# A hybrid block on one core: the front of its mixer is put in another order

## The chip, the cores and the metric

The kernel runs on one core of a Trainium2 chip. The metric is the time of one execution on the device in microseconds (us), the median of several runs. Engines: TensorE (PE; PEld is its weight load), VectorE (DVE), ScalarE (ACT), GpSimd (POOL), and SyncE (SP), which here only issues DMAs. ScalarE issues DMAs too (ACTq).

## The reference

One layer over 1024 latent and 256 context tokens, width 1024, in float32: a gated feed-forward half-step, a mixer, a second half-step, a final norm. Each is modulated by nine vectors of 1024 made from the conditioning vector. The mixer, cut to what matters:

```python
p = h @ w_in                                  # latent and context tokens
# delta-net group: 4 heads of 128
qkv = silu(centred_dwconv(p[q, k, v], conv))  # 5 taps, along the tokens
q, k = l2norm(q), l2norm(k)
beta = sigmoid(p[b]); g = -exp(a_log) * softplus(p[a] + dt_bias)
o = gated_delta(q, k, v, g, beta)             # chunked, both directions
dn = rmsnorm(o) * silu(p[z])
# attention group: 4 query heads, 2 key/value heads of 128
aq, ak = rope(rmsnorm(p[q])), rope(rmsnorm(p[k]))   # latent tokens: 2-D rotation
at = softmax(aq @ ak.T / sqrt(128)) @ av
x = x + gate * (concat(dn, at) @ w_out)
```

## The kernel before

All products are float32 built from three products of rounded parts: a weight or activation is split into a high half (`whi`, `hh..`, a ScalarE copy) and a low half (`wlo`, `hl..`, a subtraction); `load_cols(..., spare=True)` does the subtraction on GpSimd. There are two buffers for raw weights and four each for halves of 128x1024, so two weight blocks of 256 columns at a time.

The program is written in one order; the framework then orders each engine's instructions by that order and its own estimate of when operands are ready. It may issue an instruction ahead of others written earlier on the same engine. Engines and SyncE's queue then work strictly in the issued order.

The front of the mixer, in program order:

1. z rows and value rows of tokens 4 to 7 (in blocks of 128; `tok_mm`, 24 matmuls into one of two `psB` buffers; `z_out` a Silu and a store, `v_out` a copy and a store).
2. `conv_pair("k", ..)`: two heads of the convolution. A head (`conv_head`) is 24 matmuls for each of two 512-token blocks and one 256-token block into `psA` (two buffers), copied to `pp`; then five taps per segment, the first on ScalarE, four on VectorE (`ac`), Silu, and for q and k a square. Later (`pump`) a matmul with ones sums the squares, and k and v are transposed (`tk`) and stored.
3. Ten rows of 272 columns: 16 columns for beta and decay (copied by VectorE to `ba`), 256 for query heads 0 and 1 (copied to `xr` by ScalarE).
4. The second k pair; small vectors.
5. Ten turns of `stage1` (the chunks' triangular matrices `s1N`, stored to `nb_d`, `nt_d`), each with key rows for attention; the four v heads of the convolution stand before the loop and after turns 2, 4 and 7.
6. Both q pairs of the convolution, with `invert` (31 steps of two VectorE instructions, then three transposing ScalarE copies `Lb` and the stores `xx_d`) beside them.
7. Eight query rows (heads 2 and 3), `invert` going on; then eight z rows, the attention keys `k_head(0)` after the fourth.
8. Four tiles (`slot`, 128x4096) are set to zero, and `stage2_load` fills their blocks from `nt_d` and `xx_d`.
9. A new PSUM pool; `attend` and the chunk recurrence `chain` take turns.

`Rope` normalizes and rotates rows: ScalarE squares each row with a scrap tile that shares its two buffers (`t2`) with the rotation, VectorE makes the reciprocal roots and scales, GpSimd rotates with a table piece `cc` loaded for each row. It works once for four rows. `leave` issues the stores.

All through the front `ml`, the modulation run, takes 64 pieces of 256 KB (`wv`, three buffers), each multiplied and summed by VectorE into `macc`; `adv(ml, n)` writes n of them.

```python
conv_pair("k", 512, 0, lambda: adv(ml, 5))
...
rope_q = Rope(gq, aq_d, 0, FOURS)
for c in (8, 9, 0, 1, 2, 3, 4, 5, 6, 7):
...
    nc.vector.tensor_copy(ba[:, c, :], pa[:, 0:16])
...
    adv(ml, 2)
...
for pr in range(2):
    conv_pair("q", 0, pr, lambda: (adv(inv, 3), leave(2)))
```

## Time and profile before

| | us |
|---|---|
| median of 3 runs (lowest, highest) | 2449.36 (2445.76, 2452.54) |
| the profiled execution's own time | 2441.68 |
| its span, first to last instruction | 2439.9 |
| TensorE busy in the span | 2340.8 |
| VectorE, ScalarE, GpSimd busy | 1747.9, 1142.8, 865.2 |
| mean granted clock of TensorE, share of full | 0.983 |

The span is what the trace covers; the profiled execution's time has 1.8 us around it. Busy times of the engines overlap. Idle time of an engine is given with what ended it.

### The profile page before, as it was taken

To read this page: it belongs to the slowest core of one execution; us is meant where nothing else is said; L and a number is where in the kernel's file an instruction comes from. 1 tells how busy PE (TensorE), PEld (TensorE's weight loads), DVE (VectorE), ACT (ScalarE), POOL (GpSimd) and SP (SyncE) were. 2 spreads that over 40 slices of the span, in tenths; PEclk is the share of its full clock that TensorE was granted. 3 is DMA by queue.
4 is the path that set the end of the run, shared out by engine and by line. 5 is a ranking of instruction groups with operands and counts; after the bars stand their busy time and mean duration, and the time that the engine had idled before them with its cause. 6 is when DMAs were issued, how large, how long until landed. Compare 5 with 4: busy or idle time off the path is not lost. (4 is left out here: it accounts for less than half of the span.)

```text
span 2439.9 us, 35896 instructions
## 1 busy us (share of the span) xinstructions
PE 2340.8 (96%) x12917; PEld 1999.4 (82%) x12917; DVE 1747.9 (72%) x2741; ACT 1142.8 (47%) x2244; POOL 865.2 (35%) x715
## 2 busy tenths in 40 slices
PE   8999999999999999998998999899999999999998
PEld 5999788877788879877877798778877888878887
DVE  4689757887777875666777566886596546677786
ACT  4485633333343464366733754565573334234345
POOL 0000244446623342245524344521134444662330
PEclk9999999999999999999998999999999999999999
DMA  9966434345554446454433456621343234555332
GB/s 303 309 215 213 150 121 156 126 158 191 179 184 130 143 158 198 152 158 130 132 107 123 116 148 198 217 102 53 106 149 119 94 134 155 177 179 168 131 128 87
DMA packets 344976, 377.80 MB, mean 155 GB/s; under 512 B 73579, under 2 KB 249375, under 8 KB 344415
## 3 DMA queue, kind: packets, MB, share of 16 engines
q1 hardware_dynamic: 298576, 320.03, 40.6%
q10 hardware_dynamic: 46223, 55.49, 6.9%
q8 instruction: 102, 1.67, 0.3%
q14 instruction: 75, 0.61, 0.1%
HBM read 283.41 MB, written 92.01 MB: 154 GB/s over the span
## 5 line engine op out<-in xcount | busy, mean ns | idle before, releaser
L407 PE MATMUL psw<-xo,uhi 128*128 128x512 f32 x1536 | 487.5, 394 | 10.3 <-ACT k L46 5.4
L407 PEld LDWEIGHTS psw<-xo,uhi 128*128 128x128 f32 x1536 | 289.8, 189 | 77.9 <-ACT k L46 6.5
L407 PE MATMUL psw<-slot,uhi 128*128 128x512 f32 x1024 | 320.8, 391 | 3.7 <-DVE nk L49 3.4
L407 PE MATMUL psw<-xo,ulo 128*128 128x512 f32 x768 | 302.6, 394 | 0.0
L49 DVE TENSOR_TENSOR ulo<-wr,uhi 128x512 fp32r<-128x512 f32 (+1 forms) x272 | 212.1, 802 | 73.6 <-ACT uhi L46 72.9
L49 POOL TENSOR_TENSOR R<-wr 128x512 f32<-128x512 f32 (+1 forms) x68 | 98.3, 1456 | 379.7 <-DMA wr<-in_ffn_w 343.3
L407 PEld LDWEIGHTS psw<-slot,uhi 128*128 128x128 f32 x1024 | 193.1, 189 | 45.8 <-issue 4.2
L46 ACT ACTIVATE uhi<-wr 128x512 fp32r<-128x512 f32 (+1 forms) x272 | 150.5, 597 | 127.1 <-PE psw L407 85.3
L407 PE MATMUL psw<-slot,ulo 128*128 128x512 f32 x512 | 200.2, 391 | 0.0
L407 PEld LDWEIGHTS psw<-xo,ulo 128*128 128x128 f32 x768 | 144.9, 189 | 32.2
L52 DVE SCALAR_TENSOR_TENSOR macc<-wv,cs,macc 128x512 f32<-128x512 f32 x140 | 134.9, 982 | 39.5 <-DMA wv<-in_w_mod 38.5
L55 PE MATMUL psA<-hc,whi 128*128 128x256 f32 x832 | 154.0, 284 | 2.3 <-ACT sil L46 2.3
L49 POOL TENSOR_TENSOR ext<-wr 128x512 f32<-128x512 f32 (+1 forms) x68 | 95.7, 1417 | 154.6 <-DMA wr<-in_ffn_w 134.4
L46 ACT ACTIVATE whi<-wr 128x1024 fp32r<-128x1024 f32 x100 | 104.3, 1054 | 89.9 <-PE pd L55 28.2
L55 PEld LDWEIGHTS psA<-hc,whi 128*128 128x128 f32 x832 | 130.8, 191 | 3.5 <-ACT sil L46 2.6
L55 PE MATMUL psA<-hc,wlo 128*128 128x256 f32 x416 | 118.2, 284 | 7.6 <-POOL wlo L49 7.6
L49 DVE TENSOR_TENSOR wlo<-wr,whi 128x1024 fp32r<-128x1024 f32 x82 | 100.2, 1234 | 27.9 <-ACT whi L46 25.8
L49 DVE TENSOR_TENSOR ulo<-ext,uhi 128x512 fp32r<-128x512 f32 (+1 forms) x102 | 96.9, 978 | 28.9 <-ACT uhi L46 28.0
L407 PEld LDWEIGHTS psw<-slot,ulo 128*128 128x128 f32 x512 | 96.5, 188 | 20.1
L46 ACT ACTIVATE k<-k 128x512 f32<-128x512 f32 x57 | 36.0, 632 | 158.6 <-DVE k L49 158.6
L52 DVE SCALAR_TENSOR_TENSOR ac<-pp,cols,ac 128x1024 f32<-128x1024 f32 (+1 forms) x80 | 84.8, 1071 | 34.2 <-ACT ac L46 33.1
L49 DVE TENSOR_TENSOR k<-psw,k 128x512 f32<-128x512 f32 x114 | 76.8, 683 | 44.2 <-PE psw L407 42.7
(485 smaller groups left out, 6277.3 us busy)
## 6 DMA issues: line engine op xcount, KB each, us to landing
wr<-in_ffn_w SPq DMA_DIRECT2D x174, 512.0 KB, 5.2
wv<-in_w_mod SPq DMA_DIRECT2D x128, 256.0 KB, 3.2
R<-gda ACTq DMA_DIRECT2D x74, 256.0 KB, 4.7
wr<-in_ffn_w SPq DMA_DIRECT2D x32, 384.0 KB, 4.9
wr<-in_w_in SPq DMA_DIRECT2D x22, 512.0 KB, 4.4
gs<-gdb ACTq DMA_DIRECT2D x43, 256.0 KB, 4.6
gda<-gt SPq DMA_DIRECT2D x40, 256.0 KB, 2.1
gdb<-gt SPq DMA_DIRECT2D x40, 256.0 KB, 2.6
```

The source lines that it names most:

```text
L46: return nc.scalar.activation(out, in_, func, **kw)
L49: return (eng or nc.vector).tensor_tensor(out=out, in0=a, in1=b, op=op)
L52: return nc.vector.scalar_tensor_tensor(out=out, in0=a, scalar=s, in1=b, op0=op0, op1=op1)
L55: nc.tensor.matmul(out, l, r, start=start, stop=stop)
L407: nc.tensor.matmul(banks[u][key], l[:, u, k, :], r_, start=new and i == 0, stop=i == 3 * pr.kq - 1, skip_group_check=True)
```

## The change

It puts the front into another order. z rows of tokens 4 to 7 come before the value rows, and all weight loads stand earlier in the program. The second set of z rows stands between the two q pairs, the query rows of heads 2 and 3 last. Attention keys, the first query block and the zeros are written between those query rows. The rotation table stays in SBUF (half as wide, cosine and sine once per pair). `ba` is copied by ScalarE, the squares get a scrap tile of their own, two of the four zero tiles are written by ScalarE as copies with scale 0, and the value low halves of head 0 are made by VectorE. `tc.keep_in_program_order` holds each sum of `ml` behind the VectorE instruction written before it, and `beat` writes one after taps 0 and 2 of each segment.

```diff
-    aq_d = [dr.tile([P, 512], F32, name=f"aq_d{c}") for c in range(8)]
+    aq_d = [[dr.tile([P, 256], F32, name=f"aq_d{c}_{i}") for c in range(8)] for i in range(2)]
...
-                    stt(acc[b], wr, c_, acc[b], ALU.mult, ALU.add)
+                    pin(stt(acc[b], wr, c_, acc[b], ALU.mult, ALU.add))
...
+    rope = rp.tile([P, 8, 2, 64], F32, name="rope")
+    nc.sync.dma_start(rope, A["rope"])
...
-            junk = rp.tile([P, P], F32, tag="t2", name="sq", bufs=2)
+            junk = rp.tile([P, P], F32, tag="sq", name="sq")
...
-                    cc = rp.tile([P, 2, P], F32, tag="cc", name="cc", bufs=4)
-                    nc.sync.dma_start(cc, A["rope"][c].rearrange("j p e -> p j e"))
-                    t2 = rp.tile([P, 2, 64, 2], F32, tag="t2", name="t2", bufs=2)
+                    t2 = rp.tile([P, 2, 64, 2], F32, tag="t2", name="t2")
                     xv = xn.rearrange("p h (e w) -> p h e w", w=2)
-                    sv = cc[:, 1, :].rearrange("p (e w) -> p e w", w=2)
+                    co, si = (rope[:, c, i, :] for i in range(2))
                     for w in range(2):
-                        tt(t2[:, :, :, w], xv[:, :, :, 1 - w], sv[:, :, w].unsqueeze(1).to_broadcast([P, 2, 64]), ALU.mult, nc.gpsimd)
-                    tt(xn, xn, cc[:, 0:1, :].to_broadcast([P, 2, P]), ALU.mult, nc.gpsimd)
-                    tt(xn, xn, t2.rearrange("p h e w -> p h (e w)"), ALU.add, nc.gpsimd)
+                        tt(t2[:, :, :, w], xv[:, :, :, 1 - w], si.unsqueeze(1).to_broadcast([P, 2, 64]), ALU.mult, nc.gpsimd)
+                    tt(xv, xv, co.unsqueeze(1).unsqueeze(3).to_broadcast([P, 2, 64, 2]), ALU.mult, nc.gpsimd)
+                    for w, op in enumerate((ALU.subtract, ALU.add)):
+                        tt(xv[:, :, :, w], xv[:, :, :, w], t2[:, :, :, w], op, nc.gpsimd)
...
-    ml = mod_run([(q, (0,)) for q in range(10, 18)], 2, lambda: m1.tile([P, 512], F32, tag="wv", name="wv", bufs=3))
+    ml = mod_run([(q, (0,)) for q in range(10, 18)], 2, lambda: m1.tile([P, 512], F32, tag="wv", name="wv", bufs=3), tc.keep_in_program_order)
...
+                if tap in (0, 2):
+                    beat()
...
     for c in range(4, 8):
         z_out(c, tok_mm(hsel, W_z, c, 256)[:, 0:256], 0)
+    Wk0 = conv_load(512, 0)
+    for c in range(4, 8):
         v_out(c, tok_mm(hsel, W_v, c, 256)[:, 0:256])
...
-    conv_pair("k", 512, 0, lambda: adv(ml, 5))
...
+    Wk1 = conv_load(512, 1)
+    conv_pair("k", 0, Wk0, beat=lambda: adv(ml, 1))
+    W = load_cols(w_in, 2576, spare=True)
...
-        nc.vector.tensor_copy(ba[:, c, :], pa[:, 0:16])
+        act(ba[:, c, :], pa[:, 0:16], AF.Copy)
...
-    conv_pair("k", 512, 1, lambda: adv(ml, 5))
+    conv_pair("k", 1, Wk1, beat=lambda: adv(ml, 1))
+    Wv = conv_load(1024, 0)
...
-    W = load_cols(w_in, 2576, spare=True)
-    heads = []
-    for pr in range(2):
-        heads.extend(conv_heads("v", 1024, pr))
+    heads = conv_heads("v", 0, Wv, lambda: adv(ml, 1))
     before = None
-    heads.pop(0)()
     for c in range(10):
...
-        if c in (2, 4, 7):
+        if c in (0, 3, 5, 8):
             heads.pop(0)()
+        if c == 3:
+            heads = conv_heads("v", 1, conv_load(1024, 1), lambda: adv(ml, 1))
+        if c == 8:
+            Wq0 = conv_load(0, 0)
         adv(ml, 2)
+    Wz = load_cols(w_in, 1792, spare=True)
...
-    for pr in range(2):
-        conv_pair("q", 0, pr, lambda: (adv(inv, 3), leave(2)))
+    conv_pair("q", 0, Wq0, lambda: (adv(inv, 3), leave(2)))
+    Wq1 = conv_load(0, 1)
...
+    for c in range(8):
+        z_rows(c)
+        adv(inv, 2 if c % 4 else 1)
+        if c in (2, 5):
+            pump()
+    Wq = load_cols(w_in, 2320, spare=True)
+    conv_pair("q", 1, Wq1, lambda: (adv(inv, 3), leave(2)))
...
-        eng.memset(sl, 0.0)
+        if eng is nc.scalar:
+            for i in range(4):
+                act(sl[:, i, :].rearrange("p (a b) -> p a b", b=P), ones.unsqueeze(1).to_broadcast([P, 8, P]), AF.Copy, scale=0.0)
+        else:
+            eng.memset(sl, 0.0)
...
+    q0 = const.tile([P, 4, P], F32R, tag="wm", name="q0", bufs=3)
+    for c in range(8):
         leave()
         rope_q(c, tok_mm(hsel, Wq, c, 256)[:, 0:256])
...
+        if c == 0:
+            adv(inv, 3)
+            pump()
+        if c == 1:
+            run(inv)
...
+            flush()
...
+            clear(1, nc.scalar)
+            clear(3, nc.gpsimd)
+        if c == 2:
+            stage2_load(0, 2, 0)
...
+            k0 = k_head(0, lambda n: krs.pop(0), [(c, 2) for c in range(0, 10, 2)], lambda: pst("Y"), ep_tiles())
+        if c == 3:
+            q0 = q_prep(0, 0, lambda: pst("Y"), (q0[:, 0:2, :], q0[:, 2:4, :]))
+            clear(0, nc.scalar)
+            clear(2, nc.gpsimd)
+    leave(9)
     stage2_load(0, 2, 1)
...
-            split_copy(wide(0, c0, n), wide(1, c0, n), vr, nc.gpsimd)
+            split_copy(wide(0, c0, n), wide(1, c0, n), vr, nc.gpsimd if kv else None)
```

`q_prep` now takes the PSUM buffer and the place of its result, and for the first block loads by SyncE; `conv_load(c0, pr)` is `load_cols(w_in, c0 + pr * 256, spare=True)`.

## Rows read from the trace of the kernel before

**Rows 1.** The page's first part: busy us, share, instructions.
```profile
PE 2340.8 (96%) x12917; PEld 1999.4 (82%) x12917; DVE 1747.9 (72%) x2741; ACT 1142.8 (47%) x2244; POOL 865.2 (35%) x715
```
**Rows 2.** By stretches: us, busy PE, PEld, DVE, ACT, POOL; clock; DMA.
```profile
936.00:1341.40 405.40, 370.46 (x2299) 330.54 (x2297) 273.95 (x430) 196.37 (x428) 163.82 (x185) 0.95 0.47 142
1341.40:1357.60 16.20, 12.39 (x47) 8.15 (x48) 8.96 (x21) 11.74 (x30) 8.38 (x6) 0.79 0.70 134
```
**Rows 3.** TensorE's waits, 936 to 1358: us in total, times, longest.
```profile
PE psA L55 <- POOL wlo L49: 7.6, 4, 5.5
PE psY L55 <- ACT pp L46: 5.1, 2, 3.9
PE psY L1394 <- DVE kl L49: 4.1, 1, 4.1
...
PE pS L55 <- ACT qh L46: 3.4, 1, 3.4
PE psB L55 <- ACT xr L46: 3.1, 2, 2.2
...
PE psB L55 <- ACT th L46: 2.8, 1, 2.8
PE psA L55 <- ACT pp L46: 2.3, 1, 2.3
```
**Rows 4.** ScalarE's waits, 936 to 1342.
```profile
ACT sq L46 <- POOL xr L49: 21.3, 5, 9.1
ACT xr L46 <- DVE ba L1188: 19.8, 7, 5.1
```
**Rows 5.** VectorE's waits, 936 to 1342.
```profile
DVE macc L52 <- DMA wv<-in_w_mod: 30.4, 24, 7.3
```
**Rows 6.** Waits of SyncE's queue, 936 to 1342.
```profile
SPq L1067 <- POOL xr L49: 89.3, 12, 65.0
```
**Rows 7.** GpSimd in order of time, 955 to 994: start, us, what, idle before.
```profile
955.81 10.95 POOL L49 TENSOR_TENSOR wlo<-wr,whi 128x1024 fp32r<-128x1024 f32 x4 [26.07 <-ACT whi L46]
```
**Rows 8.** ScalarE's groups, 936 to 1342: count, busy us, mean ns, idle before.
```profile
L46 ACT ACTIVATE whi<-wr 128x1024 fp32r<-128x1024 f32 x18 | 18.8, 1052 | 6.4 <-PE psA L55 4.7 <-PE psB L55 1.1 <-issue 0.6
L46 ACT ACTIVATE sq<-xr 128x128 f32<-128x128 f32 x52 | 15.9, 306 | 22.1 <-POOL xr L49 21.3
...
L46 ACT ACTIVATE xr<-psB 128x256 f32<-128x256 f32 x26 | 9.8, 378 | 39.6 <-DVE ba L1188 19.8 <-PE psB L55 19.8
...
L46 ACT ACTIVATE Lb<-Xb 128x1024 f32<-128x1024 f32 x2 | 3.9, 2009 | 0.0
```
**Rows 9.** ScalarE in order of time, 1335 to 1343: a z row's Silu.
```profile
1337.12 0.38 ACT L46 ACTIVATE th<-psB 128x256 f32<-128x256 f32 x1 [2.50 <-PE psB L55]
```
**Rows 10.** GpSimd's groups, 936 to 1345.
```profile
L49 POOL TENSOR_TENSOR t<-xr,cc 128x128 f32<-128x128 f32 x48 | 28.1, 597 | 86.8 <-issue 42.3 <-DVE xr L52 29.6 <-ACT ac L46 14.8
L49 POOL TENSOR_TENSOR xr<-xr,t 128x256 f32<-128x256 f32 x24 | 21.4, 891 | 0.5
```
**Rows 11.** VectorE's groups, 936 to 1342.
```profile
L52 DVE SCALAR_TENSOR_TENSOR ac<-pp,cols,ac 128x1024 f32<-128x1024 f32 x48 | 67.2, 1400 | 22.6 <-ACT ac L46 22.2
L52 DVE SCALAR_TENSOR_TENSOR macc<-wv,cs,macc 128x512 f32<-128x512 f32 x56 | 55.3, 988 | 31.0 <-DMA wv<-in_w_mod 30.4
L52 DVE SCALAR_TENSOR_TENSOR ac<-pp,cols,ac 128x256 f32<-128x256 f32 x32 | 18.5, 577 | 11.6 <-ACT ac L46 10.9
...
L1380 DVE MEMSET slot<- 128x4096 f32 x2 | 6.9, 3472 | 1.6 <-DMA ldq<-aq_d 0.8 <-DMA z_d<-th 0.8
```
**Rows 12.** VectorE in order of time, 1323 to 1343.
```profile
1323.66 0.17 DVE L1059 TENSOR_SCALAR ssc<-ssc 128x8 f32<-128x8 f32 x1 [7.73 <-ACT sq L46]
...
1326.92 4.01 DVE L52 SCALAR_TENSOR_TENSOR xr<-xr,rsc,gq 128x128 f32<-128x128 f32 x8
```
**Rows 13.** One v head's matmuls alone, by stretches (columns of rows 2 without GpSimd).
```profile
1111.50:1125.50 14.00, 13.92 (x72) 11.74 (x72) 0.00 (x0) 0.99 (x2) 1.00 0.50 144
```
**Rows 14.** VectorE in order of time, 954 to 985.
```profile
956.79 11.30 DVE L52 SCALAR_TENSOR_TENSOR macc<-wv,cs,macc 128x512 f32<-128x512 f32 x5 [0.71 <-DMA wv<-in_w_mod]
```

More of the change, by code (lines that the diff above doesn't have):

```diff
@@ L214, in mod_vec, with mod_run @@
             tt(mods[:, b, 4 * q : 4 * q + 4], red, cols1[:, off["b_mod"] + 4 * q : off["b_mod"] + 4 * q + 4], ALU.add)
-    def mod_run(qs, ahead=2, home=lambda: const.tile([P, 512], F32, tag="wm", name="wv", bufs=3)):
+    def mod_run(qs, ahead=2, home=lambda: const.tile([P, 512], F32, tag="wm", name="wv", bufs=3), pin=lambda i: i):
         todo_ = [(q, bs, k) for q, bs in qs for k in range(KT)]
@@ L1162, in conv_heads, with conv_pair @@
         return [lambda f=f: head(f) for f in range(2)]
-    def conv_pair(kind, c0, pr, then=lambda: None):
-        for fn in conv_heads(kind, c0, pr):
+    def conv_pair(kind, pr, W, then=lambda: None, beat=lambda: None):
+        for fn in conv_heads(kind, pr, W, beat):
             fn()
@@ L1398, in k_head, with q_load, q_prep @@
         return kh, kl
-    def q_load(kv, t):
+    def q_load(kv, t, eng=None):
         ld = ep.tile([P, 2, P], F32, tag="ldq", name="ldq", bufs=3)
-        nc.scalar.dma_start(ld.rearrange("p h e -> p (h e)"), aq_d[t][:, kv * 256 : kv * 256 + 256])
+        (eng or nc.scalar).dma_start(ld.rearrange("p h e -> p (h e)"), aq_d[kv][t])
         return ld
-    Wq = load_cols(w_in, 2320, spare=True)
-    rope_q = Rope(gq, aq_d, 256, FOURS)
-    def q_rows(c):
+    def q_prep(kv, t, new_ps, home=None):
+        qh, ql = home or (ap_.tile([P, 2, P], F32R, tag=nm, name=nm, bufs=2) for nm in ("qh", "ql"))
+        ld = q_load(kv, t, nc.sync if home else None)
+        pt = new_ps()
+        for j in range(2):
+            nc.tensor.transpose(pt[:, j * P : (j + 1) * P], ld[:, j, :], ident)
+        split_copy(qh, ql, pt[:, 0:256].rearrange("p (h e) -> p h e", h=2))
+        return qh, ql
@@ L1410, in q_rows @@
+    rope_q = Rope(gq, aq_d[1], FOURS)
+    q0 = const.tile([P, 4, P], F32R, tag="wm", name="q0", bufs=3)
+    for c in range(8):
         leave()
         rope_q(c, tok_mm(hsel, Wq, c, 256)[:, 0:256])
-    def z_rows(c):
-        z_out(c, tok_mm(hsel, Wz, c, 256)[:, 0:256], 256)
-    for c in range(4):
-        q_rows(c)
-        adv(inv, 5)
-        pump()
-    run(inv)
-    Wz = load_cols(w_in, 1792, spare=True)
-    es_m3.close()
-    es_hc.close()
-    slots, es_slots = open_pool("slots", side="right")
@@ L1425, in block_kernel @@
-    slot_pool = {1: slots, 3: slots}
-    for c in range(4, 8):
-        q_rows(c)
-    clear(1, nc.vector)
-    clear(3, nc.gpsimd)
-    stage2_load(0, 2, 0)
-    flush()
-    es_m1.close()
-    slots_b, es_slots_b = open_pool("slots_b", side="right")
-    slot_pool.update({0: slots_b, 2: slots_b})
-    clear(0, nc.vector)
-    clear(2, nc.gpsimd)
-    stage2_load(0, 2, 1)
-    ep, es_ep = open_pool("ep", side="right")
-    for c in range(8):
-        z_rows(c)
-        if c > 1:
-            leave()
-        if c == 3:
-            k0 = k_head(0, lambda n: ep.tile([P, 2, P], F32, tag="ldq", name="kr", bufs=3).rearrange("p c e -> p (c e)"), [(c, 2) for c in range(0, 10, 2)], lambda: pst("Y"), ep_tiles())
+        if c == 0:
+            adv(inv, 3)
+            pump()
@@ new lines, in block_kernel @@
+        if c == 1:
+            run(inv)
+            es_m3.close()
+            es_hc.close()
+            flush()
+            es_m1.close()
+            slots, es_slots = open_pool("slots", side="right")
+            slots_b, es_slots_b = open_pool("slots_b", side="right")
+            slot_pool = {1: slots, 3: slots, 0: slots_b, 2: slots_b}
+            ep, es_ep = open_pool("ep", side="right")
+            clear(1, nc.scalar)
+            clear(3, nc.gpsimd)
+        if c == 2:
+            stage2_load(0, 2, 0)
+            krs = [rp.tile([P, 256], F32, tag="zt", name="kr", bufs=3) if i < 3 else ep.tile([P, 2, P], F32, tag="ldq", name="kr", bufs=3).rearrange("p c e -> p (c e)") for i in range(5)]
+            k0 = k_head(0, lambda n: krs.pop(0), [(c, 2) for c in range(0, 10, 2)], lambda: pst("Y"), ep_tiles())
@@ L1625, in kv_head @@
             nc.scalar.dma_start(vr.rearrange("p (c e) -> p c e", e=P), av_d[c0 : c0 + n, :, kv * P : (kv + 1) * P].rearrange("c p e -> p c e"))
-            split_copy(wide(0, c0, n), wide(1, c0, n), vr, nc.gpsimd)
+            split_copy(wide(0, c0, n), wide(1, c0, n), vr, nc.gpsimd if kv else None)
         return *k_, *v_
-    def q_prep(kv, t):
-        qh = ap_.tile([P, 2, P], F32R, tag="qh", name="qh", bufs=2)
-        ql = ap_.tile([P, 2, P], F32R, tag="ql", name="ql", bufs=2)
-        ld = q_load(kv, t)
-        pt = tps()
-        for j in range(2):
-            nc.tensor.transpose(pt[:, j * P : (j + 1) * P], ld[:, j, :], ident)
-        split_copy(qh, ql, pt[:, 0:256].rearrange("p (h e) -> p h e", h=2))
-        return qh, ql
     def scores_into(kvt, q, es):
@@ L1736, in attend @@
                 rounds(scores_into(kvt, q, es), pend)
-                q = q_prep(kv, t + 1) if t < 7 else None
+                q = q_prep(kv, t + 1, tps) if t < 7 else None
                 pend = values(kv, t, kvt, es)
```

37 lines of the change are left out of this document (18 added, 19 removed).

## The prediction

> **What bounds the kernel now.** I read the page first: its first part says which engine is full. TensorE is busy for 2340.8 of 2439.9 us [rows 1], so only about 99 us of the span are idle time at all, and a change that leaves every product in place can win no more than idle time and time at a low clock. The change touches one stage: from the z and value rows (about 936 us) to the first attention step. I cut that stage out with the view by stretches. From 936.0 to 1341.4, where the first score matmul starts, TensorE is busy for 370.46 of 405.40 us: 34.9 us idle. Its mean granted clock is 0.95 there, that is, some stretches at 1.2 GHz among 2.4 GHz: (1 - 0.95) x 405.4 = 20.3 us lost at most. In the 16.2 us after that another 3.8 us are idle, at 0.79 [rows 2]. So about 60 us, 2.4% of the time, is all that can be had.
>
> Third, TensorE's own waits in that stage [rows 3]. The reader is to see that no single wait rules: the low halves of split weights (`wlo`, GpSimd) cost 7.6 us in 4 waits, the squares of a conv head (`pp`) 5.1, the low half of the attention keys (`kl`) 4.1, the first query block (`qh`) 3.4, the copies out of the two `psB` buffers 3.1 (`xr`) and 2.8 (`th`), a conv bank 2.3. Last, the waits of the others, since they make those: ScalarE waits 21.3 us for GpSimd's rotation before it may square, and 19.8 us for VectorE's small copy `ba` before it may copy `xr` [rows 4]; VectorE stands 30.4 us before data of the modulation weights [rows 5]; SyncE's queue stands 89.3 us at the table loads `cc` [rows 6].
>
> **Weights asked for earlier.** No load and no split is added; they change places. The longest `wlo` wait, 5.5 us, is that of the second value pair. In the new order its load stands after turn 3, two turns before its use, instead of at its use: I count 5.5 as gone and keep the other 2.1 of 7.6. In return the first query pair's load stands only one turn ahead of its use. Its buffers come free with the last value head, and then two `whi` at 1.05 and two `wlo` at about 2.7 run as a pipeline of some 1.05 + 2 x 2.7 = 6.5 us [rows 7, 8], of which the turn's key rows cover 2.9 (0.38 + 2.50 us between two such rows) [rows 9]. So a new wait of 0 (the turn's other products cover the rest) to 3.6; I take 1.8.
>
> **`ba` on ScalarE, squares with a tile of their own.** Ten copies of 16 columns move from VectorE to ScalarE. The view has no such copy there; by the copies of 256 columns they cost at most 0.38 each [rows 8], 3.8 in all, beside the 41.1 us of waits that ScalarE loses by the two edits [rows 4]. `xr` then needs no VectorE, and the 3.1 goes; the 2.3 of the conv bank is ScalarE's arrears from that loop, and goes too: 5.4 in all (3.1 if the arrears have another cause).
>
> **z rows between the query heads.** Eight z rows (24 matmuls, one Silu, one store on ScalarE's queue each) move from the end to between the two pairs of query heads: same number, other place. The squares of a head come late because five taps, Silu and Square must run after its last product; eight rows of 2.9 us are there to be run meanwhile. The longer wait, 3.9 of 5.1, goes; the last pair still has only two query rows behind it, so I keep 1.2. What was covered by the z rows, and now isn't, comes below.
>
> **Rotation table, low halves, first query block.** 24 table loads leave SyncE's queue, and with them the 89.3 us; the store of a row and the modulation loads then stand behind GpSimd alone. GpSimd does per row two products of 128, one of 256 and two half sums instead of one whole: 4 x 0.60 + 0.89 against 2 x 0.60 + 2 x 0.89 [rows 10], 0.3 us more, 7 us over 24 rows, on an engine off the path. The first query block is loaded, turned and split before the new PSUM pool: its 3.4 goes. The value low halves of head 0 go from GpSimd to VectorE: under 1 us each (`macc`, a 512-column sum, takes 0.99 [rows 11]).
>
> **Zeros by ScalarE.** Two memsets of 3.47 us leave VectorE [rows 11]; eight copies of 1024 columns come to ScalarE, between 1.05 (a plain copy) and 2.0 (the `Lb` copies, 2.009) each [rows 8]. I take 1.05, the same shape: 8.4 us. They stand in the last six query rows, where TensorE has 6 x 2.9 = 17.3 us of work and ScalarE now 8.4 + three `Lb` copies 6.0 + six `xr` 2.3 + twelve squares 3.7 + six copies of keys and queries 2.3 = 22.7. It is over by 5.4. But only `xr` and the key copies hold TensorE, so I let the waits of this place, 2.8 and 4.1, stay as they are, and count the 5.4 as the upper end.
>
> **The end without its cover.** Before, the second half of the query rotation ran under z rows. Now it comes after the last row: its chain on VectorE takes 1326.92 + 4.01 - 1323.66 = 7.3 us [rows 12], and VectorE must give the first score maxima in the same time; four rows of 3.3 us on GpSimd follow, and the row stores and the second part of the slot loads wait behind them on SyncE. Between 0 (the maxima go first) and 7.3; I take the middle, 3.7. The slot loads have the first two attention steps as cover.
>
> **Sums pinned between taps.** No instruction is added; each of up to four sums per head of k or v now stands behind a tap. A head of k takes 4 x 1.40 + 4 x 0.58 + 4 x 0.99 = 11.9 us of VectorE [rows 11], and 13.9 of TensorE [rows 13]. So it is covered as long as no sum waits for its data: 0.
>
> Rows for a weighing: beside four `wlo` on GpSimd (10.95 us), five `macc` on VectorE took 11.30, so 2.26 each against 0.99 in the mean [rows 7, 11, 14]. The Trainium skill says why, in "SBUF — State Buffer", section "Who interferes with whom": a VectorE instruction with two SBUF inputs and a GpSimd instruction that reads SBUF can't run side by side; the one that comes second is held for the whole of the other. By that rule a sum pinned between taps can be held by GpSimd and hold back taps that wait on nothing else. By the mean of the rows the sum above has 0 here, by the slowed rows 12.4 us of TensorE (worked out below). I go by the mean, since it already holds the slowed ones, and carry the rest as a rival.
>
> **The sum.** Gone: 5.5 + 5.4 + 3.9 + 3.4 = 18.2. New: 1.8 + 3.7 = 5.5. Net 12.7 us of idle time. I let the loss by low clock shrink in proportion to the idle time (20.3 us beside 34.9, 0.58 for each), so 7.4 more: 20.1. The profiled execution took 2441.68, with 1.8 outside the span; 2441.7 - 20.1 = 2421.6. It lies 7.7 under the median of the runs, 2449.36, so against the median I expect **2429**.
>
> **Rivals.**
> *Nearly all goes.* ScalarE, relieved of 41.1 us, also catches up at `kl` and `th`, and no new wait shows: 7.6 + 5.1 + 5.4 + 3.4 + 6.9 = 28.4, x 1.58 = 45: 2404. For it: those two waits too end with ScalarE's arrears. Against: `Lb` and the zeros stand there.
>
> *Given back beside GpSimd.* If each pinned sum takes 2.26, a k pair needs 2 x (11.9 + 4 x 1.27) = 34.0 us of VectorE against 27.8 of TensorE: 6.2 per pair, 12.4 for both, x 1.58 = 19.6. That eats the gain: 2449, no change. (It is what the rule of the Trainium skill above would do to this kernel.) For it: the rows weighed above, and GpSimd's rotation of the first query rows falls beside the second k pair. Against: VectorE has slack before and after, and two buffers each of `pp` and `ac`. The same time comes out if the end gives back both its upper bounds (5.4 + 7.3 + 3.6 = 16.3 against 18.2: 2446), or if the order in which instructions are issued hardly follows the new program order.
>
> *Slower: the pinned sums wait for data.* VectorE works in order. A sum that waits w for its 256 KB holds the taps behind it, and a k head needs 11.9 + 4w against 13.9. Four k heads then cost 4 x (4w - 2.0) x 1.58. With w = 2: 38 us, so 2429 + 38 = 2467. It turns the sign from about w = 1.6 on. For it: in 24 waits VectorE has stood 1.27 in the mean and 7.3 at the longest [rows 5]. Against: there the sums ran back to back, as fast as data came; with two taps of 1.40 between them three buffers have time to fill, and the table loads are out of the queue.
>
> **How the numbers follow.** Forecast (10 to 35 us faster) 0.60; nearly all 0.14; given back 0.15; slower 0.11. About 0.3%, 7.3 us, is what can be told from no change: faster 0.74, same 0.15, slower 0.11. The range reaches from the second case's 2404 to just past "no change", 2450, and leaves out the slower case and a part of the others.
>
> **What would show it.** `sq` behind `xr` and `xr` behind `ba` gone from ScalarE's waits; no wait for `wlo` above 4 us; no wait for `qh`; no table loads; fewer falls of the clock in the stage, and TensorE idle there for about 22 instead of 34.9 us. Wrong if VectorE's waits for modulation data lie between taps with `psA` idle, if the last query rows wait for `xr` behind zeros, or if the first scores wait for VectorE longer than the z rows saved.

## The result, and the profile after

| | before | after |
|---|---|---|
| median of 15 runs each (lowest, highest), us | 2450.19 (2438.93, 2453.95) | 2462.72 (2454.34, 2469.66) |
| ratio, 95% interval | | 1.0055 (1.0045 to 1.0065) |
| the profiled execution's time, us | 2441.68 | 2459.11 |

The change makes the kernel 0.55% slower, some 13 us; the forecast, 2429, was some 20 us faster. The page's first part, to be held against [rows 1]:

```profile
PE 2346.4 (95%) x12917; PEld 2000.1 (81%) x12917; DVE 1740.8 (71%) x2732; ACT 1145.3 (47%) x2256; POOL 869.1 (35%) x736
```

TensorE has the same 12917 products, and the span is 17.4 us longer (2457.3 us after 2439.9): the loss is idle time (110.9 us after 99.1) and low clock (the same products took 5.6 us more). By stretches (columns as in [rows 2]): the front up to the first score matmul, the next 16.2 us, and all of the attention and recurrence up to the last output matmul (`po`):

```profile
938.60:1343.40 404.80, 367.82 (x2299) 327.11 (x2297) 257.21 (x398) 197.00 (x430) 158.86 (x178) 0.94 0.45 132
1343.40:1359.60 16.20, 8.23 (x21) 5.74 (x22) 11.71 (x29) 7.48 (x22) 12.93 (x25) 0.50 0.65 153
1343.40:1703.40 360.00, 331.25 (x2381) 294.25 (x2382) 258.55 (x640) 208.02 (x555) 140.06 (x147) 0.96 0.48 143
```

The front is as long as it was (404.8 us; 405.7 before, measured in the same way, from the first z row), with 37.0 us idle. Behind it, in 16.2 us, TensorE issues 21 matmuls where it issued 47, at a granted clock of 0.50, the 1.2 GHz level, where it was 0.79 [rows 2]. The last stretch took 348.9 before, 11.1 less. The front and this stretch together are 10.2 us longer; the other 7 us of the span lie ahead of them and behind them, where the change hardly reaches, and are taken here as scatter of one execution. So two things have to be explained: why the front gained nothing, and why the attention starts badly. TensorE's waits from 938 to 1368, against [rows 3]:

```profile
PE psD L211 <- DVE macc L52: 22.1, 5, 9.1
PE pS L55 <- ACT e L46: 8.0, 3, 4.5
PE psY L55 <- ACT pp L46: 5.1, 2, 3.0
PE pS L55 <- ACT xr L46: 3.4, 1, 3.4
...
PE psY L1418 <- DVE kl L49: 1.4, 1, 1.4
PE psB L55 <- ACT xr L46: 0.7, 1, 0.7
```

The waits for `wlo`, `qh`, `th` and the conv bank are gone, those for `kl` and `xr` are small. In their place stands one that the kernel before doesn't have: `psD`, line 211, the four transposes with which TensorE begins to fold a finished modulation sum (`mod_vec`), waiting for the last sum `macc` (three of the five waits are in the query rows, two in the value heads). Here is VectorE around the longest, the 9.1 us that end at 1036.9:

```profile
1022.28 2.99 DVE L52 SCALAR_TENSOR_TENSOR macc<-wv,cs,macc 128x512 f32<-128x512 f32 x3
1029.53 2.87 DVE L52 SCALAR_TENSOR_TENSOR macc<-wv,cs,macc 128x512 f32<-128x512 f32 x3 [4.25 <-DMA wv<-in_w_mod]
1036.13 0.75 DVE L52 SCALAR_TENSOR_TENSOR macc<-wv,cs,macc 128x512 f32<-128x512 f32 x1 [3.74 <-DMA wv<-in_w_mod]
```

VectorE itself waits twice for the weights. SyncE's queue over the same time says why:

```profile
1015.75 0.33 SPq L225 DMA_DIRECT2D wv<-in_w_mod  x1
1022.24 4.24 SPq L1076 DMA_DIRECT2D aq_d<-xr  x2
1026.57 1.36 SPq L225 DMA_DIRECT2D wv<-in_w_mod  x3
1028.93 4.19 SPq L1076 DMA_DIRECT2D aq_d<-xr  x2
```

Between 1015.75 and 1026.57 no weight is asked for: the queue stands at stores of query rows that GpSimd is still rotating. The order of waiting is then GpSimd, store, load, sum, transposes, and behind the transposes all of TensorE.

At the attention's start ScalarE's row of work is this:

```profile
1334.81 3.89 ACT L46 ACTIVATE slot<-ones 128x1024 f32<-128x1024 f32 x4
...
1338.87 3.88 ACT L46 ACTIVATE slot<-ones 128x1024 f32<-128x1024 f32 x4
...
1342.95 0.63 ACT L46 ACTIVATE xr<-psB 128x256 f32<-128x256 f32 x2
1343.35 0.40 ACTq L1648 DMA_DIRECT2D e<-av_d  x1
...
1346.91 0.63 ACT L46 ACTIVATE vh<-e 128x512 fp32r<-128x512 f32 x1 [1.43 <-DMA e<-av_d]
1347.55 1.28 ACT L46 ACT_TABLE_LOAD   x1
1348.85 0.69 ACT L46 ACTIVATE e<-pS,nm 128x512 f32<-128x512 f32 x1
...
1356.73 0.47 ACT L46 ACTIVATE e<-pS,nm 128x256 f32<-128x256 f32 x1 [5.34 <-DVE nm L1664]
```

and VectorE's, some 12 us of it:

```profile
1346.33 0.69 DVE L1664 TENSOR_REDUCE nm<-pS 128x1 f32<-128x512 f32 x1 [0.59 <-PE pS L55]
1346.94 0.16 DVE L1061 TENSOR_SCALAR ssc<-ssc 128x8 f32<-128x8 f32 x1
...
1351.45 3.71 DVE L52 SCALAR_TENSOR_TENSOR xr<-xr,rsc,gq 128x128 f32<-128x128 f32 x8
1355.08 1.28 DVE L49 TENSOR_TENSOR vl<-e,vh 128x512 fp32r<-128x512 f32 x2
1356.28 1.01 DVE L1664 TENSOR_REDUCE nm<-pS 128x1 f32<-128x256 f32 x2
```

The zeros (each 0.97 us) hold the copies of the last two query rows until 1343; the squares, and with them the rotation's chain, come late; and that chain stands from 1346.94 to 1355.1, the first `vl` within it, between the second and the third score maximum `nm`. TensorE waits 4.5 us for the exponentials meanwhile.

Another 3.0 of its 8.0 us for `e` come earlier and have another source. The loads of the value rows (`e<-av_d`) stand on ScalarE's queue behind the copies of the last query rows, and the first is issued with the first score matmul (1343.36); ScalarE then waits for them and loads a table before the first exponential, though the second maximum has been ready since 1347.0. In the kernel before the first of these loads was issued 4.2 us ahead of the first score matmul (1341.36), and the first exponential came 3.3 us behind it, where it now comes 5.5 behind:

```profile
1337.13 0.38 ACTq L1625 DMA_DIRECT2D e<-av_d  x1
...
1344.66 0.69 ACT L46 ACTIVATE e<-pS,nm 128x512 f32<-128x512 f32 x1
```

### The profile page after: what moved, and what is told of

Same layout as the page of the kernel before. It is cut to its first block, busy times and chain, and to the rows that moved or that the text cites. A ratio compares the mean times of both kernels' runs of the same rounds, so it can differ in the third digit from the quotient of the medians.

```text
span 2457.3 us, 35870 instructions
## 1 busy us (share of the span) xinstructions
PE 2346.4 (95%) x12917; PEld 2000.1 (81%) x12917; DVE 1740.8 (71%) x2732; ACT 1145.3 (47%) x2256; POOL 869.1 (35%) x736
## 4 chain that ended last, share of the span: by engine, by line
PE 71%; DVE 14%; ACT 5%; DMA 4%; issue 3%; POOL 2%; ACTq 0%; SPq 0%; DVEq 0%; POOLq 0%
PE psw L407 43%; PE psA L55 7%; PE pd L55 6%; PE psw L55 3%; PE psB L55 2%; PE po L55 2%; PE psY L55 2%; PE pS L55 2%; DVE macc L52 2%; DVE ac L52 1%; PE psY L861 1%; PE pt L1691 1%; DMA wv<-in_w_mod 1%; DVE ulo L49 1%; PE psD L55 1%
## 5 line engine op out<-in xcount | busy, mean ns | idle before, releaser
L407 PE MATMUL psw<-xo,uhi 128*128 128x512 f32 x1536 | 489.3, 396 | 10.5 <-DVE k L49 5.3
L407 PEld LDWEIGHTS psw<-xo,ulo 128*128 128x128 f32 x768 | 145.6, 190 | 32.5
L52 DVE SCALAR_TENSOR_TENSOR ac<-pp,cols,ac 128x1024 f32<-128x1024 f32 (+1 forms) x80 | 94.3, 1184 | 59.7 <-ACT ac L46 58.8
```

The costliest lines, as they stand in the source:

```text
L52: return nc.vector.scalar_tensor_tensor(out=out, in0=a, scalar=s, in1=b, op0=op0, op1=op1)
L407: nc.tensor.matmul(banks[u][key], l[:, u, k, :], r_, start=new and i == 0, stop=i == 3 * pr.kq - 1, skip_group_check=True)
```

## The experiments

Each ratio is to the kernel before, with its 95% interval. A difference between two runs carries both intervals, some 0.2% or 5 us. The table behind them has two lengths of each profiled execution. One execution's lengths scatter by up to some 7 us (the fronts of runs 6, 9, 11 and 13, which differ only in what becomes of the last four query rows, are 400.0, 393.0, 392.9 and 393.5), so the ratios decide.

**1. No pin.** The sums stay written between the taps.

```diff
-    ml = mod_run(..., tc.keep_in_program_order)
+    ml = mod_run(...)
```

> The changed kernel, but the modulation sums are not pinned; they are still written between the taps. Theory A (the pin is what costs): TensorE's waits for the last pinned sum of a vector at its transposes (22.1 us in five waits in the changed kernel) go, and with them about half as much lost by low clock: 22 to 33 us less, a part of which other waits take back, so 2430 to 2441 us and a ratio to the kernel before of 0.992 to 0.997. Theory B (those waits stand where TensorE would have waited anyway, for conv heads or rows): other waits of the same size take their place and the time stays at 2458 to 2466, ratio 1.003 to 1.007. Neither expects a change at the first attention step, where the first output matmul comes 24.5 us after the first score matmul.

Measured: 1.0010 (0.9994 to 1.0026). No wait at the transposes is left, and the 0.45% (11 us) is half of what theory A named: other waits take a part back, above all `psD` for `s1N` (8.4 us) and a conv bank for `pp` (6.0). So the pin makes most of the loss; taking it away brings no gain over before. The gain is in the front (396.8 us after 404.8); the start of the attention stays as it was.

**2. Zeros by VectorE.** `clear(1, nc.vector)`, `clear(0, nc.vector)` in place of `nc.scalar`.

> The changed kernel, but the two zero tiles are written by VectorE with memset again instead of by ScalarE. Theory A (ScalarE's eight copies of zeros, 7.8 us, hold the last two copies of query rows and the squares behind them): the first scores start about 3.4 us earlier, the squares and the last rotation too, and the first output matmul comes 4 to 7 us earlier: 2456 to 2459, ratio 1.0025 to 1.004. Theory B (the lost cover of the last rotation rules, whoever writes the zeros; VectorE's memsets of 3.5 us stand in the same place): 2460 to 2466, ratio 1.004 to 1.0065.

Measured: 1.0042 (1.0024 to 1.0060), between the two; the interval covers both, and the 1.0055 of the change. The `xr` wait before the first scores is gone, but the waits for `e` grew from 8.0 to 13.9 us, and the first output matmul came later, not earlier. VectorE's memsets stand in the place of the zeros.

**3. No pin, z rows last.** Query rows of heads 2 and 3 between the query pairs, z rows at the end (the key rows get other buffers).

```diff
     for c in range(8):
-        z_rows(c)
+        leave()
+        rope_q(c, tok_mm(hsel, Wq, c, 256)[:, 0:256])
         adv(inv, 2 if c % 4 else 1)
...
-        rope_q(c, tok_mm(hsel, Wq, c, 256)[:, 0:256])
+        z_rows(c)
         if c == 0:
```

> As the kernel without the pin, and with query rows and z rows exchanged: the query rows stand between the two pairs of query heads, the z rows last, beside the keys, the first query block and the zeros. Theory A (the missing cover of the last rotation costs the 9 us by which the changed kernel's first output matmul falls behind): VectorE's chain for the last rotation no longer stands between the first scores, and the time is 6 to 14 us under the kernel without the pin: 2420 to 2432, ratio 0.988 to 0.993. Theory B (the attention step is late for another reason, ScalarE's zeros or the slot loads): within 3 us of the kernel without the pin. A third way: the query rows between the pairs ask more of ScalarE and VectorE than z rows do, and the squares of the heads come late again by some 4 to 5 us, which eats half of it.

Measured: 1.0037 (1.0020 to 1.0054), slower than without the exchange. The start of the attention heals (18.5 us from the first score to the first output matmul), but the third way is larger than stated: the wait for the squares of a query head is 11.4 us. Its taps on VectorE, between the rotation's chain and `invert`:

```profile
1301.48 4.18 DVE L52 SCALAR_TENSOR_TENSOR xr<-xr,rsc,gq 128x128 f32<-128x128 f32 x8
1305.58 1.55 DVE L52 SCALAR_TENSOR_TENSOR ac<-pp,cols,ac 128x1024 f32<-128x1024 f32 x1
1307.05 1.10 DVE L49 TENSOR_TENSOR tmb<-Lb,Xb 128x660 f32<-128x660 f32 x1
```

**4. Stores by GpSimd, pinned.** `outs.append(... nc.gpsimd.dma_start(self.dst[c], ...))` in place of `nc.sync`.

> The changed kernel, pinned, but the stores of rotated rows are issued by GpSimd, which rotates them, instead of by SyncE's queue, so that no modulation load stands behind a store that waits for GpSimd. Theory A1 (the last pinned sums are late since their loads stand behind such stores): the 9.1 us wait of TensorE at the transposes in the ten query rows shrinks to under 3, and the time falls by 6 to 14 us, to 2449 to 2457. Theory A2 (they are late since VectorE must work through taps first): the 9.1 stays or a part of it, the time stays at 2459 to 2466. The waits of 5.1 and 4.5 us in the value heads, where VectorE's taps stand ahead of the sum, stay in both.

Measured: 1.0011 (0.9995 to 1.0027). The queue now asks for twelve weights without a break:

```profile
1014.24 20.52 SPq L225 DMA_DIRECT2D wv<-in_w_mod  x12
```

The 9.1 us wait in the query rows is 3.4, not quite under 3, and the time falls by as much as A1 says. Of the waits in the value heads, which were to stay, the first is 4.7 us and the second fell to 1.8; in all the transposes still wait 15.3 us, in six. But the time isn't gained where A1 has it: the front is 404.0 us after 404.8, and from the first score to the last output matmul it is 354.0 after 360.0. There the first matmul of the recurrence (`pd`) comes 9.7 us after the first score instead of 16.1.

**5. The pin alone, in the kernel before.** Only `pin(stt(...))` and the argument for it.

> The kernel before with the pin alone: its modulation sums stay where its program writes them (five after each key head, two after each turn), but none may pass another VectorE instruction. Theory A (a pinned sum comes late and TensorE stands at its transposes, in any order of the front): waits at the transposes appear as in the changed kernel, 5 to 20 us, and the time rises by 5 to 15: 2453 to 2463, ratio 1.002 to 1.006. Theory B (the pin only costs together with the new places between the taps): ratio 0.999 to 1.002.

Measured: 1.0058 (1.0043 to 1.0072): the whole loss of the change, without any of its other parts. Its waits to the first scores and just behind them:

```profile
PE psD L211 <- DVE macc L52: 12.5, 4, 5.0
...
PE psB L55 <- ACT xr L46: 6.5, 2, 5.6
PE psB L55 <- ACT th L46: 5.9, 2, 3.8
```

The transposes' share is 12.5 (and 3.3 more that ended with a ScalarE instruction); the waits for row copies (`xr`, `th`) are 6.5 us longer than in [rows 3].

**6. No pin, stores by GpSimd.** The edits of 1 and 4 together.

> The changed kernel without the pin and with the stores of rotated rows issued by GpSimd. Each alone gave about 11 us back. Theory A (the two give back in different places: without the pin the front is 8 us shorter up to the first score matmul; with the stores on GpSimd the slot loads land earlier and the time from the first score matmul to the last output matmul is 6 us shorter): they add up to some 14 to 20 us less than the changed kernel, 2443 to 2449, ratio 0.997 to 0.9995. Theory B (both heal the same late sums): no more than one alone, 2450 to 2454, ratio 1.001 to 1.002.

Measured: 0.9983 (0.9970 to 0.9995), 2441.6 us: they add up, theory A. Without the pin the stores are worth 0.27% (1 to 6), with it 0.44% (the change to 4): most of what they give has nothing to do with the pin.

**7. A small last turn.** As 6, and the last query rows in groups of four, three and one.

```diff
-    rope_q = Rope(gq, aq_d[1], FOURS)
+    rope_q = Rope(gq, aq_d[1], [(0, 1, 2, 3), (4, 5, 6), (7,)])
```

> As the kernel without the pin and with stores by GpSimd, and the last query rows are rotated in groups of three and one instead of four, so that only one row is left after the last query product: the same small VectorE steps as for four, but two scalings instead of eight, and one row instead of four on GpSimd. Theory A (the uncovered last rotation on VectorE holds the first score maxima): VectorE's chain between the first scores shrinks by 2.7 us and GpSimd's rows by 10, and the time from the first score matmul to the first output matmul by 3 to 6 us; 3 to 6 less than the kernel without the pin and with stores by GpSimd. Theory B (ScalarE's zeros or the slot loads rule there): within 2 us of it. A cost: eleven small VectorE steps more, 2.2 us, under cover.

Measured: 1.0010 (0.9998 to 1.0022), not faster than 6. It doesn't tell the theories apart: the third group needs a third `xr` tile where there are two, so the last row's copy waited 10.5 us for a store, and the scores with it (6.8).

**8. No sums between taps.** As 1, and five sums after each key head: `conv_pair("k", 0, Wk0, lambda: adv(ml, 5))`, value heads without `beat`.

> The changed kernel without the pin, and with five sums written after each key head as before instead of one after two taps of each segment: the rest of the new order alone. Theory A (the sums between the taps still cost something without the pin, they stand ahead of taps on VectorE): the two waits for conv banks that the kernel without the pin has (6.0 us, squares and copies of a head late) shrink, and it is 2 to 6 us faster than that kernel: 2446 to 2450. Theory B (the framework moves unpinned sums wherever it likes, whatever the program says): within 2 us of it, 2450 to 2454.

Measured: 1.0005 (0.9992 to 1.0019), within 2 us of 1, theory B by the time. By the waits theory A is half right: those for conv banks shrink from 6.0 to 1.0 us, and a new one of 10.2 for ScalarE's small vectors takes their place.

**9. The last turn left out.** As 6, with an early return for rows 4 to 7 of heads 2 and 3.

> As the kernel without the pin and with stores by GpSimd (2441.6 us, 0.9983), and the normalization and rotation of the last four query rows are left out altogether: their rows are stored raw (VectorE's 7 us chain between the first scores and 13 us of GpSimd are gone, the data are not the reference's). Theory A (the uncovered turn holds the first score maxima): the first output matmul comes 5 to 9 us earlier after the first score matmul (23.9 us there) and the time is 2432 to 2437, ratio 0.9945 to 0.9965. Theory B (ScalarE's zeros hold the last rows, or the recurrence's start takes the time): within 2.5 us of 2441.6.

Measured: 0.9960 (0.9944 to 0.9976). 0.23% less than 6, 5.6 us, at the lower end of theory A and hardly clear of the two intervals. Its mechanism is only in part what the profile shows: the first output matmul comes 2.9 us earlier, not 5 to 9, and TensorE's waits for `e` at the start are hardly shorter (8.4 in run 6):

```profile
PE pS L55 <- ACT e L46: 7.4, 5, 5.1
```

The 5.1 us are those behind the loads of the value rows: the first exponential comes 6.3 us after the first score, with the first two maxima ready after 2.5. So of the 8 to 9 us by which the start falls behind the kernel before, 5.0 are there without the turn (20.7 against 15.7).

**10. Zeros by GpSimd.** As 6, `clear(1, nc.gpsimd)`, `clear(0, nc.gpsimd)`.

> As the kernel without the pin and with stores by GpSimd, and all four zero tiles are written by GpSimd (two more memsets of 3.5 us there), none by ScalarE. Theory A (ScalarE's 7.8 us of zeros hold the last copies of rows, 3.9 us before psB, and the squares, and so the last turn): the last turn starts some 5 us earlier and 4 to 7 us are gained: 2435 to 2438. Theory B (GpSimd is now late with the first four rotations and the slot loads stand behind its zeros): the recurrence's first matmul comes later and nothing is gained or up to 5 us lost: 2441 to 2447.

Measured: 1.0013 (0.9999 to 1.0027), 0.30% or 7 us slower than 6, a little more than B says. The waits at `psB` for the last rows' copies `xr` fell from 4.7 us (run 6) to 0.7, so the zeros did hold ScalarE; but the attention's start takes 31.1 us.

**11 and 13. The turn deferred.** As 6; rows 4 to 7 are stored raw, and in the fourth attention step loaded, normalized, rotated and stored. In 13 the first VectorE step of it is kept in program order.

```diff
                 rounds(scores_into(kvt, q, es), pend)
+                if (kv, t) == (0, 3):
+                    rope_q.late()
+                    leave(9)
```

> As the kernel without the pin and with stores by GpSimd, and the last four query rows are stored raw and normalized and rotated later, beside the fourth attention step, where nothing waits for them for over 100 us: the reference's result in full. Theory A: most of what leaving the turn out gains stays, 2433 to 2438; GpSimd's 13 us and VectorE's 8 us more beside the fourth step cost TensorE under 3 us there. Theory B (VectorE is the attention steps' bound, so the chain costs the same there): 2439 to 2444.

> As the kernel with the deferred last turn, and the first VectorE step of that turn is kept in program order, so that the whole turn is issued in the fourth attention step and not between the first scores (there, in the version without this, VectorE stood 9.2 us at the rows' way back from DRAM). Theory A (the uncovered turn is what the attention's start loses): like the kernel that leaves the turn out, 0.9945 to 0.9975. Theory B (VectorE has no room in the fourth step either): 0.998 to 1.001.

Measured: 1.0019 (1.0006 to 1.0031) and 1.0008 (0.9994 to 1.0023). In 11 the framework issued the late turn at the old place, where VectorE stood 9.2 us at the rows' way back, so 11 says nothing on the theories. In 13 the order is as meant: its first output matmul comes 19.6 us after the first score, as early as with the turn left out (20.7). Then it is given back. The stretch from 75 to 125 us after the first score, in 13 and then in 9:

```profile
1410.00:1460.00 50.00, 41.16 (x299) 37.94 (x298) 32.52 (x84) 20.28 (x50) 30.44 (x43) 0.90 0.46 130
```

```profile
1409.50:1459.50 50.00, 48.45 (x393) 45.61 (x392) 31.77 (x79) 26.61 (x70) 15.73 (x15) 1.00 0.52 136
```

7.3 us of TensorE less where the turn now lies. By the time it is theory B, but not by its reason, that VectorE has no room: VectorE is busy for 32.5 of these 50 us, 31.8 in 9. It stands 7.2 us at the rows' way back from DRAM, as in 11, and TensorE behind it; the two lines are VectorE's and TensorE's:

```profile
1430.65 0.61 DVE L52 SCALAR_TENSOR_TENSOR xq<-xq,rsc,gq 128x128 f32<-128x128 f32 x2 [7.17 <-DMA xq<-aq_d]
1431.91 0.58 PE L55 MATMUL po<-el,vh 128*128 128x256 f32 x1 [6.84 <-DVE el L49]
```

So 13 prices the turn together with its reloaded rows; what it would cost there with the rows at hand was not run.

**14. Deferred, zeros by VectorE.** As 13 with the edit of 2.

> As the kernel with the turn deferred and kept, and the two zero tiles of ScalarE are written by VectorE, which then has nothing else to do there. Theory A (ScalarE's zeros hold the copies of the last query rows, 3 to 4 us of TensorE at psB): those waits go and 2 to 6 us are gained on the kernel with the turn deferred and kept. Theory B (the zeros hold nothing that ends last, or VectorE's 7 us hold the keys' low halves): within 2 us of it or slower.

Measured: 1.0036 (1.0024 to 1.0049), slower; the keys' low halves wait (2.6 us) and the scores wait 14.5 for `e`, since the first rows' scalings (4.15 us) and the second memset (3.47) stand before the first maxima.

**12 and 15. Late transposes, pinned.** The four transposes of a sum are written after the next vector's fourth piece; 15 has the stores by GpSimd too.

```diff
-                if i:
+                if i and not lag:
                     next(gen, 0)
...
+            if lag and k == lag and old:
+                next(old, 0)
```

> The changed kernel, pinned, but the four transposes of a finished sum are written three pieces of the next vector later. Theory A (what the pin costs is TensorE standing at transposes that come too early for their sum): the 22.1 us of waits there shrink to under 5 and the time comes near that of the kernel without the pin, ratio 0.999 to 1.003. Theory B (the pin costs through VectorE's order, taps and small vectors behind sums that wait for data): ratio 1.004 to 1.007 as in the changed kernel, with waits elsewhere.

> The changed kernel, pinned, with stores of rotated rows by GpSimd and the transposes of a sum three pieces later. Theory A (the pin's cost is loads behind stores and transposes too early, nothing else): as the kernel without the pin and with stores by GpSimd, 0.997 to 1.000, waits at the transposes under 4 us in all. Theory B (a pinned sum also holds VectorE's taps and small vectors): 1.001 to 1.004.

Measured: 1.0027 (1.0013 to 1.0040) and 1.0022 (1.0007 to 1.0036). In 12 the waits at the transposes are 7.8 us in two, not under 5; the larger, 6.4, is at the sixth of the eight sets, and why it stays was not found. The late transposes take back 0.28 of 0.55%, what theory A allows, and the front is 397.8 us, nearly that of run 1. But with the stores by GpSimd, late transposes bring nothing more: 15 isn't better than 4, and stays 0.39% over the same kernel without the pin (6), with 8.0 us of waits at the transposes. That is nearer to theory B.

**16 to 18. Parts on the kernel before.** 16: stores by GpSimd. 17: `act(ba[:, c, :], ...)` and the squares' own tile. 18: 17, the resident table and 16, in the old order of rows.

> The kernel before with one change that is no part of the new order: the stores of rotated rows are issued by GpSimd instead of SyncE's queue. It tells whether the 0.17% that the new order without the pin gains with these stores belongs to the new order. Theory A (the stores help any order, since loads of modulation weights and slots stand behind them): 2438 to 2443, ratio 0.997 to 0.999. Theory B (the stores help only where the slot loads stand behind the last, uncovered rows): 0.999 to 1.001.

> The kernel before with two parts of the change alone: the 16 columns for beta and decay are copied by ScalarE instead of VectorE, and the squares have a scrap tile of their own. The prediction's step for them: 5.4 us of TensorE's waits (copies of rows 3.1, a conv bank 2.3), with the clock's share 8.5: 2437 to 2441, ratio 0.9965 to 0.998. The rival (ScalarE's waits for these were idle time that nothing waited for at the end): 0.999 to 1.001.

> The kernel before, in its old order of rows, with the parts of the change that move nothing (the copies by ScalarE, the scrap tile, the resident half-wide table) and the stores of rotated rows by GpSimd; not the pin, not the new order, not the zeros by ScalarE. If the order of rows and the pin are what the change loses by, this keeps the gains without giving any back: 2430 to 2440, ratio 0.994 to 0.998, the fastest with the full result. The rival (these parts gain nothing by themselves, what the new order without the pin gains in the front comes from the z rows and the earlier loads): 0.999 to 1.001.

Measured: 16 1.0022 (1.0009 to 1.0034); 17 0.9995 (0.9980 to 1.0010); 18 **0.9966 (0.9953 to 0.9980)**, 2437.3 us, the fastest with the full result. 16 lies above both of its theories, 17 within its rival, 18 within its forecast. The largest wait of TensorE in 16, then in 17:

```profile
PE psB L55 <- ACT th L46: 13.2, 1, 13.2
```

```profile
PE psY L1135 <- ACT smalls L46: 11.4, 2, 10.5
```

In 16 the 13.2 us (2.8 before) lie behind a ScalarE that stands 9.7 us before a square, whose scrap tile shares its buffers with the rotation; GpSimd, rotating, now issues the stores between its rows (0.58 us each). With a scrap tile of its own, in 18, no such wait is left. In 17 the waits for `xr` and the conv bank are gone as foreseen, and a new one of 10.5 us stands behind ScalarE's small vectors. That the tile is what lets 18 gain where 16 loses fits these waits and wasn't shown by a run of its own; neither the tile nor the table was run by itself.

Lengths in the profiled executions: the front (first z row to first score matmul), and from there to the first output matmul.

| | ratio | front, us | to first output, us |
|---|---|---|---|
| before | 1 | 405.7 | 15.7 |
| after | 1.0055 | 404.8 | 24.5 |
| 1 no pin | 1.0010 | 396.8 | 23.5 |
| 2 zeros by VectorE | 1.0042 | 404.6 | 29.6 |
| 3 no pin, z rows last | 1.0037 | 407.0 | 18.5 |
| 4 stores by GpSimd | 1.0011 | 404.0 | 22.9 |
| 5 pin alone, in before | 1.0058 | 415.5 | 15.9 |
| 6 no pin, stores by GpSimd | 0.9983 | 400.0 | 23.7 |
| 9 last turn left out | 0.9960 | 393.0 | 20.7 |
| 10 zeros by GpSimd | 1.0013 | 390.4 | 31.1 |
| 12 late transposes | 1.0027 | 397.8 | 24.4 |
| 13 turn deferred | 1.0008 | 393.5 | 19.6 |
| 15 late transposes, stores by GpSimd | 1.0022 | 403.9 | 23.8 |
| 18 parts, in before | 0.9966 | 394.2 | 15.8 |

## Why the prediction was wrong, point by point

**The step that failed: "Sums pinned between taps: 0".** It cost the taps' VectorE time against TensorE's, and made the cover depend on the data being there. Run 5 puts its price at 0.58%, 14 us; run 1 at 0.45%, 11 us, within the change. The condition did fail, since sums waited for data, but the place was another than all rivals named. Not taps were held back before a conv bank: TensorE, which works in order too, stood at the transposes that end a sum, in the query rows as well as in the heads. Those four short matmuls are nowhere in my working, because in the kernel before TensorE has no wait at them [rows 3]. Nor has it one in runs 1 and 6, without the pin: there the transposes begin at least 0.2 us behind their sum, some of them over 10 us, and in the change the five sets that wait begin 0.1 us behind it.

**Its cause, as far as shown.** Transposes that come before their sum take part of it: written later (run 12), they give back 0.28% and 7 us of the front. Loads behind row stores do lengthen the longest wait (the queue's rows; 9.1 to 3.4 us in run 4), but what run 4 gains, it gains mostly behind the front, and without the pin too; their share in the pin's price isn't clear of the intervals. With both mended and the pin kept (run 15) 0.39% stays over the same kernel unpinned. That this rest is VectorE's order, small vectors and scalings behind sums, fits the row waits of run 5 and was not shown.

**What the pin doesn't explain.** Between the forecast of 2429 and the result lie 34 us, and the pin is 11 of them. Without it (run 1's profile against that of before) the front is 8.9 us shorter, where the working has (18.2 - 1.8) x 1.58 = 25.9; and from the first score to the last output matmul it is 12.0 longer, where the working has 3.7 x 1.58 = 5.8. Of the waits that were to go all but the squares' did go; counting each at its full length is the second thing that failed, since others stood ready behind them (run 1: 8.4 and 6.0 us).

**The rival "Slower: pinned sums wait for data"** had the right sign and cause, and by luck nearly the right time, 2467; its price, by taps and conv banks, is not what happened. By its own formula the sign turns at a w of 1.3, not 1.6: 4 x (4 x 1.3 - 2.0) x 1.58 is about the 20.1 of the gain.

**"The end without its cover", 3.7 of 0 to 7.3.** The first output matmul comes 8.8 us later after the first score (24.5 against 15.7). Leaving the turn out gives 2.9 us of that back, and 5.6 in all (run 9). The term has the turn within its bounds; what it had at nothing is the loads of the value rows, which lost their place ahead of the first score together with the z rows. No run moved them, so their price is not shown; with the turn left out 5.0 us stay. The zeros come on top: I kept the waits "as they are" and put 5.4 at the upper end; the zeros made a new 3.4 us wait for `xr`, and pushed the chain behind the second maximum. "The maxima go first" was true of two out of three.

**What was right.** Weights earlier: the 7.6 us for `wlo` are gone (5.5 expected), and the new wait of 1.8 didn't come. `qh`, 3.4: gone. `ba`, `xr` and the conv bank: 5.4 expected, 4.7 gone in the change; but run 17 shows that the same waits, taken away alone, are worth nothing that can be measured, since another stands ready behind them. `th` and `kl` lost 5.5 that I hadn't counted.

**z rows between the heads: 3.9 of 5.1.** Failed: two waits for squares, 3.0 and 2.1 us, are still there. Run 3 shows that the z rows do something all the same: with query rows in that place the wait is 11.4.

**The clock's share.** With little idle time gained it had nothing to follow; the mean in the front is 0.94 after 0.95.

**The rule weighed in the prediction.** By the Trainium skill, "SBUF — State Buffer", section "Who interferes with whom", GpSimd's reads would hold VectorE's sums between the taps. No run takes that apart; the rows: the taps took 1.52 us in the mean, 1.40 before [rows 11], the sums 0.94 after 0.99: of the two, only the taps are slower, by 48 x 0.12 = 5.8 us of VectorE, spread over a front where it is idle for 147.6 us. That isn't the place of the loss.

```profile
L52 DVE SCALAR_TENSOR_TENSOR ac<-pp,cols,ac 128x1024 f32<-128x1024 f32 x48 | 73.0, 1520 | 32.7 <-ACT ac L46 32.2
L52 DVE SCALAR_TENSOR_TENSOR macc<-wv,cs,macc 128x512 f32<-128x512 f32 x56 | 52.5, 937 | 21.9 <-DMA wv<-in_w_mod 21.4
```

## What to carry to other kernels

When an instruction is pinned in the order of its engine, follow its result to its last reader: an engine that works in order and reads it stands still with everything behind, and that price is not in the pinned engine's own budget. A wait removed is worth what is left when the next one behind it is counted: the same 5.4 us were nothing that can be measured by themselves (run 17), and with other parts beside them the gain was 8 us (run 18). Before work is put last, ask which idle engine will run its tail, and what its old place had given cover to: here the last rotation, but also the loads of the value rows. Work put off needs its data at hand; the rotation put off to the fourth attention step gave its gain back while VectorE stood at the reload of its rows.

## What was not expected of the hardware

A VectorE instruction on 128x8 elements, 0.16 us long in the kernel after, took 3.77 us in run 13 and 7.23 in run 14 (3.77 in run 9 and 3.78 in run 11 too). GpSimd's memsets of the zero tiles ran at the time. VectorE, then GpSimd, in run 13:

```profile
1319.67 3.77 DVE L1076 TENSOR_SCALAR ssc<-ssc 128x8 f32<-128x8 f32 x1 [0.84 <-ACT sq L46]
```

```profile
1319.88 3.53 POOL L1421 MEMSET slot<- 128x4096 f32 x1
```

and in run 14, with two memsets one behind the other:

```profile
1315.54 7.23 DVE L1076 TENSOR_SCALAR ssc<-ssc 128x8 f32<-128x8 f32 x1 [0.85 <-ACT sq L46]
```

```profile
1315.75 6.99 POOL L1421 MEMSET slot<- 128x4096 f32 x2
```

It ends when the memsets end (1323.44 and 1323.41; 1322.77 and 1322.74); its record begins 0.21 us ahead of theirs. The same page and section of the Trainium skill says that a tensor_scalar can take the pair of ports that VectorE shares with GpSimd, and that whoever has the pair keeps it for the whole instruction while the other is blocked; the rows agree in the length of the block. They don't show who was first, and with two memsets the block lasted for both. In run 10 the same step took 3.30 us beside a memset, at the head of the chain that holds the score maxima. No run here shows what the start would be without it.
